# Two kinds of side work on ScalarE queued behind each tile's eviction, and one pair's late output operands behind the next pair's first copy

## The chip, the cores and the metric

The kernel runs on one NeuronCore of a Trainium2 chip. A core has a matmul engine (TensorE, PE), three engines for elementwise work (VectorE or DVE, ScalarE or ACT, GpSimd or POOL), a queue for DMA issues (SyncE, SP) and 16 DMA engines. Each engine takes its instructions in one fixed order and waits on semaphores for what the others make. Matmuls write to PSUM, eight banks of 2 KB per partition; the other engines carry ("evict") results from there to SBUF. The metric is the device time of one execution, in microseconds (us).

## The reference

One layer of a token mixer on two groups, 2048 latent tokens and 128 context tokens, width 1024. Each group is normalised and modulated, multiplied by one combined input projection and split over three branches (a gated delta rule over chunks, a spatial gating unit, Fourier mixing); the branches are gated, projected and merged:

```python
def mixer(xn, w_in, conv_w, a_log, dt_bias, ...):
    proj = jnp.einsum('btd,de->bte', xn, w_in)
    qkv, beta, dec, z_a, u_b, v_b, z_b, x_c, z_c, gates = jnp.split(proj, points, axis=-1)
    qkv = short_conv(qkv, conv_w).astype(jnp.float32)        # 3 taps, then SiLU
    q, k, v = jnp.split(qkv, 3, axis=-1)
    beta = jax.nn.sigmoid(beta...)
    g = -jnp.exp(a_log) * jax.nn.softplus(dec + dt_bias)     # log-decays
    o, s_f, s_b = delta_bidir(q, k, v, g, beta, s0_f, s0_b)  # needs exp(gam_i - gam_j)
    ...
    pb = jnp.einsum('btnw,nwd->btnd', br, w_branch)
    gt = jax.nn.sigmoid(gates.reshape(B, T, N_BRANCH, D_MODEL))
    merged = jnp.einsum('btnd,btnd->btd', gt, pb)
    return jnp.einsum('btd,de->bte', merged, w_out), s_f, s_b
```

## The kernel before

Products are made in float16 pairs: an operand x is held as a high and a low half (xh, xl; whi, wlo), and one product is three matmuls, high by high, low by high and high by low. The tokens stay in SBUF with channels on the partitions; 2176 tokens are cut into four tiles of 512 and one of 128 (TBS).

The stage that the change touches first makes q, k and v: a loop over 12 column tiles (ct) of the projection. For each of the five token tiles, `gemm_T` issues 24 matmuls (8 blocks of the contraction, three products each) into a PSUM bank, and L986 evicts the bank to `raw` on ScalarE at high priority. The banks are taken in turn from two pools of three (ps_d, ps_mm), so six evictions can be outstanding before TensorE has to wait. Behind the five tiles stands the column tile's convolution: one tap on ScalarE (L993), two on VectorE (L994, L995), a sigmoid in four pieces on ScalarE (L998), products on GpSimd (L999), a store (L1000), and for the q and k columns a square with a sum (L1002).

A column tile's weights come through a chain of their own: a DMA into wst (two buffers), the sum of squares on ScalarE (L317), its cast wscb on VectorE (L265), a matmul with ones, the scales on VectorE (L279 to L281), the high half whi on ScalarE (L329) and the low half wlo on VectorE (L330).

Beside this run two generators whose results the stage itself doesn't read:

- `decays()` makes the decay table `tok` out of the projection bdp (L838 to L872, with exponentials and a logarithm on ScalarE at L854, L859 and L861), its cumulative sums with a few matmuls on TensorE (which read tok), transposed copies of them (gr, L893) that are written to memory (gamR), and then 17 decay rows of 128x1024: loaded from gamR, two operations on VectorE (L924, L925), an exponential on ScalarE (L912) and a store. `pace` steps it as tiles are issued.
- `token_sums()` makes sums and differences of token blocks for the merge at the end of the program (products with seven instead of eight multiplications): additions on GpSimd and VectorE (L956 to L962), four casts to float16 on ScalarE (L965), the remainders (L966), and stores. One set has sums of 512 columns (sg, st), the other two stretches of 512 and 64 (sgs, sts); the program holds 32 casts of 512 and 16 of 64.

A list scheduler sets each engine's order from the program's order, priorities and readiness as it reckons them; `tc.issue_after(ins)` is an edge by which everything issued under it stands behind `ins` on that engine's queue.

Much later, the merge runs over eight pairs of column blocks (`last_merge`, L2081). A pair's first bank R is copied by ScalarE at L2129 with high priority; `held_back` holds the previous pair's last operands (pa, made by `quarters` at L935 and L936), and `step()` issues them when the third unit of the current pair begins.

Of the kernel before, what the change touches and what calls it, by code (L numbers as in the profile page):

```python
# [14 lines left out]
AF = mybir.ActivationFunctionType  # L15
# [180 lines left out]
def hybrid_flow_kernel(ctx: ExitStack, tc: tile.TileContext, x_prompt, x_sample, state_delta, c, c_ctx, w_ada,  # L196
# [628 lines left out]
    def decays():  # L825
# [83 lines left out]
            return row  # L909

        def flush(t, row):
            A.activation(row, row, AF.Exp)  # L912
            A.dma_start(decD[t], row.rearrange("p d h i -> p d (h i)"))

        xb = [None]
# [30 lines left out]
    def token_sums(*which):  # L946


        for p_ in which:
            a0, b0, cn, _ = QUADS[p_]  # L950
            a, b = slice(a0, a0 + cn), slice(b0, b0 + cn)
            for k in range(4):
                own, sg, st_ = (ep, "sg", "st") if cn == 512 else (a1p, "sgs", "sts")
                f11, f12, f21, f22 = [sb(own, [P, cn], sg, bufs=4) for _ in range(4)]
                for on, f, kk, ts in ((G, f21, k, b), (V, f11, k, a), (G, f22, k + 4, b), (G, f12, k + 4, a)):
                    on.tensor_tensor(f, xh[:, kk, ts], xl[:, kk, ts], ALU.add)  # L956
                yield 1
                V.tensor_tensor(f22, f21, f22, ALU.add)
                G.tensor_tensor(f21, f11, f21, ALU.subtract)
                yield 1  # L960
                V.tensor_tensor(f11, f22, f11, ALU.subtract)
                V.tensor_tensor(f12, f12, f11, ALU.subtract)  # L962
                for i, f in enumerate((f22, f11, f21, f12)):
                    st = sb(own, [P, 2, cn], st_, F16, bufs=3)
                    A.copy(st[:, 0], f)  # L965
                    (V if i % 2 else G).tensor_tensor(st[:, 1], f, st[:, 0], ALU.subtract)  # L966
                    SY.dma_start(sD[p_][:, i, :, k, :], st)
                    yield 1

    beside, small_sums = token_sums(1, 0), token_sums(2)  # L970
    flip = [0]
    pace.start(decays(), 6.0)
    for ct in range(12):
        w = getw(1, 2 if ct < 6 else min(4, 15 - ct))
        for half in range(1):
            raw = sb(a1p, [P, LP], "raw")
            G.memset(raw[:, 0:1], 0.0)
            G.memset(raw[:, NS + 1:NS + 3], 0.0)
            G.memset(raw[:, LP - 1:LP], 0.0)
            for t0, tn in TBS:  # L980
                flip[0] ^= 1
                ps = bank(ps_d if flip[0] else ps_mm, [P, tn])
                gemm_T(ps, w, 0, xh[:, :, t0:t0 + tn], xl[:, :, t0:t0 + tn])
                o = t0 + 1 if t0 < NS else t0 + 3
                with tc.high_priority():
                    A.activation(raw[:, o:o + tn], ps, AF.Copy, scale=w.inv)  # L986
                pace.tick(tn / 100)
                if ct:
                    next(beside if tn == 512 else small_sums, 0)
                    if tn < 512:  # L990
                        next(small_sums if ct > 4 else beside, 0)
            y = sb(a1p, [P, LP - 2], "cy")
            A.activation(y, raw[:, 0:LP - 2], AF.Copy, scale=convw(0, ct))  # L993
            V.scalar_tensor_tensor(y, raw[:, 1:LP - 1], convw(1, ct), y, ALU.mult, ALU.add)  # L994
            V.scalar_tensor_tensor(y, raw[:, 2:LP], convw(2, ct), y, ALU.mult, ALU.add)  # L995
            for c0 in range(0, LP - 2, CQ):
                c1 = min(c0 + CQ, LP - 2)
                A.activation(raw[:, 1 + c0:1 + c1], y[:, c0:c1], AF.Sigmoid)  # L998
                G.tensor_tensor(y[:, c0:c1], y[:, c0:c1], raw[:, 1 + c0:1 + c1], ALU.mult)  # L999
            G.dma_start(qkvD[ct], y)  # L1000
            if ct < 4 or ct > 7:
                A.activation(raw[:, 1:LP - 1], y, AF.Square, accum_out=vqs[:, ct:ct + 1])  # L1002
# [1078 lines left out]
    def last_merge(i, p_, w, after, ending):  # L2081


        a0, b0, cn, _ = QUADS[p_]
        a, b = slice(a0, a0 + cn), slice(b0, b0 + cn)
        js = (i, i + 4)
        mr = [sb(orp, [P, 2 * cn], "mr", bufs=4) for _ in js]
        for t, j in zip(mr, js):
            SY.dma_start(t, mD[j][:, a0:a0 + 2 * cn])
        tokens = lambda k, ts: [x[:, k:k + 4, ts] for x in x2]  # L2090
        small = p_ == 1
        if small:
            c0, d0, cs, _ = QUADS[2]
            c, d = slice(c0, c0 + cs), slice(d0, d0 + cs)
            pm = sb(orp, [P, 2, 2 * cs], "pm")
            for n_, j in enumerate(js):
                SY.dma_start(pm[:, n_], mD[j][:, c0:c0 + 2 * cs])
            p7 = bank(ps_x, [P, 7, cs])
        unit = [0]

        def step():
            if unit[0] == 2 and held_back:
                held_back.pop()()
            after(unit[0])
            unit[0] += 1

        def multiply(ps, w_, ts, fresh, n_, sum_=None):
            part(ps, w_, [sums[sum_, p_][:, l] for l in range(2)] if sum_ else tokens(*ts[0]), fresh)
            if small:
                part(p7[:, n_], w_, [sums[sum_, 2][:, l] for l in range(2)] if sum_ else tokens(*ts[1]))  # L2110
            step()

        def gated(n_, ts, c_):
            ps = bank(ps_d, [P, cn])
            part(ps, w.branch[n_], [o16[:, l, :, ts] for l in range(2)])
            with tc.high_priority():
                V.scalar_tensor_tensor(c_, ps, bi_[:, js[n_]:js[n_] + 1], c_, ALU.mult, ALU.mult)
            m_ = mr[n_][:, ts.start - a0:ts.stop - a0]
            G.tensor_tensor(m_, m_, c_, ALU.add)
            step()  # L2120
            return m_

        if not small:
            c = d = None
        R = bank(ps_mm, [P, cn])
        multiply(R, w.b11, ((0, a), (0, c)), True, 0)
        p1 = sb(ep, [P, cn], "sg", bufs=4)
        with tc.high_priority():
            A.copy(p1, R)  # L2129
        Y = bank(ps_mm, [P, cn])  # L2130
        multiply(Y, w.t2, None, True, 1, 1)
        u2 = sb(ep, [P, cn], "st", bufs=3)
        total(u2, Y, p1)
        multiply(R, w.b21, ((4, a), (4, c)), False, 2)
        c11 = sb(ep, [P, cn], "sg", bufs=4)
        sigmoid(c11, R, w)
        multiply(Y, w.t3, None, False, 3, 2)
        u3 = sb(ep, [P, cn], "st", bufs=3)
        total(u3, Y, p1)
        X = bank(ps_mm, [P, cn])  # L2140
        multiply(X, w.t1, ((0, b), (0, d)), True, 4)
        total(u3, X, u3)
        sigmoid(u3, u3, w)
        m1a = gated(0, a, c11)
        multiply(Y, w.t4, ((4, b), (4, d)), False, 5)
        total(p1, Y, p1)
        sigmoid(p1, p1, w)
        m2b = gated(1, b, u3)
        multiply(X, w.b22, None, False, 6, 3)
        total(u2, X, u2)  # L2150
        sigmoid(u2, u2, w)
        if ending:
            ending()
        m1b = gated(0, b, p1)
        quarters(i, b0, m1b, m2b)
        if small:
            q_ = sb(ep, [P, 7, cs], "sg", bufs=4)
            r_ = sb(ep, [P, 4, cs], "st", bufs=3)
            A.copy(q_.rearrange("p n c -> p (n c)"), p7.rearrange("p n c -> p (n c)"))
            for out, x, y in ((r_[:, 0], 0, 2), (q_[:, 1], 0, 1), (q_[:, 3], 1, 3), (r_[:, 1], 3, 5), (r_[:, 3], 3, 4), (q_[:, 4], 1, 4),  # L2160
                              (r_[:, 2], 4, 6)):
                G.tensor_tensor(out, q_[:, x], q_[:, y], ALU.add)
            sigmoid(r_.rearrange("p n c -> p (n c)"), r_.rearrange("p n c -> p (n c)"), w)
        m2a = gated(1, a, u2)
        held_back.append(lambda: quarters(i, a0, m1a, m2a))
        if small:
            ps = bank(ps_x, [P, 2, 2 * cs])
            for n_ in range(2):
                part(ps[:, n_], w.branch[n_], [o16[:, l, :, c0:c0 + 2 * cs] for l in range(2)])
            for n_ in range(2):  # L2170
                g_ = r_[:, 2 * n_:2 * n_ + 2].rearrange("p n c -> p (n c)")
                V.scalar_tensor_tensor(g_, ps[:, n_], bi_[:, js[n_]:js[n_] + 1], g_, ALU.mult, ALU.mult)
                G.tensor_tensor(pm[:, n_], pm[:, n_], g_, ALU.add)
                SY.dma_start(mD[js[n_]][:, c0:c0 + 2 * cs], pm[:, n_])
# [37 lines left out]
        SY.dma_start(gp[1], gateD[0:1, :].to_broadcast([P, D]))  # L2212
        scale_gate(gp[1], gp[1], winv)

    held_back = []
    for n_, (p_, i) in enumerate(order):
        nxt = pair_weights(order[n_ + 1][1], n_ > 2) if n_ < 7 else None

# [261 lines left out]
```

## Time and profile before

| | us |
|---|---|
| median of three runs | 2196.15 (2189.08 to 2197.21) |
| profiled execution, its own time | 2190.18 |
| its span | 2188.4 |
| mean granted clock of TensorE | 0.981 |
| ACT table loads of the decays' exponentials (L912) | 3 of 1.283 |
| qkv stage, first matmul of the second tile to the end of its last | 144.67 to 452.8 |

The span is the time from the first to the last instruction; busy shares are of it. In a group or timeline row, L251 is the helper that records every matmul of a product, so rows of that line are told apart by their tiles (`b<-xh,wlo` is the high half of the tokens by the low half of the weights into a bank). `[9.23 <-DVE tok L872]` behind a row says that the engine was idle for 9.23 us before it, and which instruction ended that.

### The profile page before, as it was taken

Reading aid. Unit: us, or ns where it says so; the run is one execution under the profiler, and the core shown is the slowest. Engines: PE = TensorE matmul, PEld = TensorE weight load, DVE = VectorE, ACT = ScalarE, POOL = GpSimd, SP = SyncE. Lnnn points to the kernel's source line nnn. Section 1 sums busy time; section 2 is a strip of 40 time slices with the busy share of each in tenths; the row PEclk is TensorE's granted clock in tenths of the full one; section 3 lists DMA queues with packets and bytes.
Section 4 is the critical chain, followed back from the end, with each engine's and each line's share of the span. In section 5 each row is a group of like instructions: output and inputs, shape, how many; then the busy total and the mean of one; then the engine's idle time right before and its main releaser. Section 6 shows DMA issues by size and latency. Waiting matters only on the chain.

```text
span 2188.4 us, 43365 instructions
## 1 busy us (share of the span) xinstructions
PE 2081.8 (95%) x16169; PEld 1190.6 (54%) x16169; DVE 1432.0 (65%) x2988; ACT 1116.4 (51%) x2525; POOL 965.4 (44%) x1178
## 2 busy tenths in 40 slices
PE   7997799999999999999899999999999998999997
PEld 4453344455555587768556655565565454444443
DVE  6667994448876777555667565766666567676345
ACT  5545675656565665355555455665665445222112
POOL 0346663324565655543423242345454435333454
PEclk9998899999999999999999999999999999999999
DMA  8523862237777575244657565776766785885862
GB/s 344 218 90 124 265 237 101 100 111 236 250 240 245 183 236 152 69 136 135 191 189 225 159 215 173 226 234 211 224 199 199 259 277 199 317 278 186 302 220 89
DMA packets 266211, 440.13 MB, mean 201 GB/s; under 512 B 47608, under 2 KB 148752, under 8 KB 262928
## 3 DMA queue, kind: packets, MB, share of 16 engines
q1 hardware_dynamic: 213488, 336.27, 47.4%
q0 software_dynamic: 12688, 57.04, 7.0%
q10 hardware_dynamic: 39824, 44.05, 6.0%
q8 instruction: 127, 2.08, 0.4%
q14 instruction: 84, 0.69, 0.1%
HBM read 276.61 MB, written 160.65 MB: 200 GB/s over the span
## 4 chain that ended last, share of the span: by engine, by line
PE 46%; DVE 9%; DMA 7%; issue 3%; ACT 3%; POOL 3%; SPq 0%; ACTq 0%; POOLq 0%; DVEq 0%
PE b L251 45%; DMA st<-br 2%; POOL E L1164 1%; DMA wst<-in_w_blk_dram 1%; DVE XB L1163 1%; DMA ei<-XB 1%; DVE big L1750 1%; DVE pa L936 1%; DMA br<-o 0%; DMA big<-pa 0%; DMA tw<-slot 0%; ACT big L1749 0%; DVE o L1297 0%; PE b L1065 0%; DMA wo<-slot 0%
## 5 line engine op out<-in xcount | busy, mean ns | idle before, releaser
L251 PE MATMUL b<-xh,whi 128*128 128x512 f16 (+2 forms) x1792 | 603.5, 347 | 14.7 <-ACT sg L2129 3.7
L251 PE MATMUL b<-xh,wlo 128*128 128x512 f16 (+2 forms) x1792 | 601.8, 347 | 11.3 <-DVE wlo L330 11.3
L251 PE MATMUL b<-xl,whi 128*128 128x512 f16 (+2 forms) x1792 | 604.0, 347 | 0.0
L251 PEld LDWEIGHTS <-whi 128*128 128x128 f16 x3872 | 348.4, 98 | 344.8 <-issue 34.7
L251 PEld LDWEIGHTS <-wlo 128*128 128x128 f16 x1936 | 189.8, 98 | 186.9 <-DVE wlo L330 12.5
L251 PE MATMUL b<-big,bhi 128*128 128x512 f16 (+1 forms) x960 | 252.7, 348 | 2.0 <-ACT big L1749 1.2
L251 PE MATMUL b<-big,blo 128*128 128x512 f16 (+1 forms) x480 | 162.8, 347 | 0.0
L251 PEld LDWEIGHTS <-xh 128*128 128x128 f16 x1512 | 119.7, 98 | 31.0 <-issue 1.6
L1164 POOL TENSOR_TENSOR E<-E,XB 128x31 f32<-128x31 f32 (+15 forms) x155 | 95.1, 613 | 76.2 <-DVE XB L1163 62.3
L251 PEld LDWEIGHTS <-bhi 128*128 128x128 f16 x960 | 86.8, 98 | 76.7 <-issue 2.8
L1237 POOL COPY T<-ES 32x256 f16<-32x256 f16 x68 | 30.7, 451 | 190.4 <-DMA ES<-ei 174.6
L999 POOL TENSOR_TENSOR cy<-cy,raw 128x545 f32<-128x545 f32 (+1 forms) x48 | 66.8, 1415 | 100.7 <-ACT raw L998 100.7
L251 PE MATMUL b<-whi,xl 128*128 128x128 f16 x544 | 94.5, 221 | 0.0
L251 PE MATMUL b<-whi,xh 128*128 128x128 f16 x544 | 94.5, 221 | 0.0
L251 PE MATMUL b<-wlo,xh 128*128 128x128 f16 x544 | 94.5, 221 | 0.0
L251 PEld LDWEIGHTS <-xl 128*128 128x128 f16 x824 | 74.7, 98 | 14.9
L1344 POOL TENSOR_TENSOR skn<-skn,ed 128x512 f32<-128x512 f32 x34 | 37.5, 1103 | 99.6 <-DMA skn<-kv 99.5
L1163 DVE TENSOR_TENSOR XB<-XB,E 128x31 f32<-128x31 f32 (+15 forms) x155 | 54.7, 353 | 40.8 <-POOL E L1164 39.8
L251 PEld LDWEIGHTS <-big 128*128 128x128 f16 x480 | 46.8, 98 | 60.1 <-DMA big<-pa 3.2
L330 DVE SCALAR_TENSOR_TENSOR wlo<-wst,wsc,whi 128x1024 f16<-128x1024 f32 x44 | 59.3, 1349 | 27.7 <-ACT whi L329 27.4
L251 PE MATMUL b<-xh,big 128*128 128x512 f16 x280 | 74.8, 379 | 2.2 <-DMA big<-pa 2.2
L1787 POOL TENSOR_TENSOR mrow<-mrow,sg 128x512 f32<-128x512 f32 (+1 forms) x40 | 48.3, 1211 | 61.2 <-DVE sg L1786 32.7
(578 smaller groups left out, 4805.0 us busy)
## 6 DMA issues: line engine op xcount, KB each, us to landing
wst<-in_w_blk_dram SPq DMA_DIRECT2D x58, 512.0 KB, 4.9
pa<-pa POOLq DMA_DIRECT2D x16, 896.0 KB, 5.2
qkv<-cy POOLq DMA_DIRECT2D x12, 1089.0 KB, 5.3
st<-br SPq DMA_DIRECT2D x48, 256.0 KB, 4.3
big<-pa SPq DMA_DIRECT2D x12, 896.0 KB, 8.6
dc<-dec SPq DMA_DIRECT2D x17, 512.0 KB, 6.1
kq<-qkv SPq DMA_DIRECT2D x34, 256.0 KB, 5.5
kv<-tok POOLq DMA_DIRECT2D x17, 512.0 KB, 4.9
```

The costliest lines, as they stand in the source:

```text
L251: newest[0] = PE.matmul(out, l, r, start=start, stop=stop, skip_group_check=reopened)
L330: w.low = V.scalar_tensor_tensor(w.lo, st, s, w.hi, ALU.mult, ALU.subtract)
L936: V.scalar_tensor_tensor(lo, src, s, hi, ALU.mult, ALU.subtract)
L999: G.tensor_tensor(y[:, c0:c1], y[:, c0:c1], raw[:, 1 + c0:1 + c1], ALU.mult)
L1163: V.tensor_tensor(t3, X3[:, 0:k, k:k + 1].to_broadcast([P, k, n_]), E3[:, k:k + 1, k:32].to_broadcast([P, k, n_]), ALU.mult)
L1164: G.tensor_tensor(E3[:, 0:k, k:32], E3[:, 0:k, k:32], t3, ALU.subtract)
L1237: G.tensor_copy(T16[rows(a0, b), :, :, b], ES[0:32, :, 2 * a0 + b, :, wT])
L1344: G.tensor_tensor(h3(kn_), h3(kn_), bc(ed[:, d, t, :], P), ALU.mult)
L1750: V.scalar_tensor_tensor(o16[:, 1, g, t0:t0 + tn], st, s, o16[:, 0, g, t0:t0 + tn], ALU.mult, ALU.subtract)
L1787: G.tensor_tensor(mr, mr, sg, ALU.add)
```

## The change

Three edges are added; no instruction of the computation is added or removed.

- The exponential of a decay row (`flush`) stands behind the newest eviction of the qkv stage at the time when the program issues it.
- So does each of the 48 casts of the token sums.
- The previous pair's held-back operands stand behind the copy of the current pair's first bank.

```diff
         def flush(t, row):
-            A.activation(row, row, AF.Exp)
+            with tc.issue_after(evicted[0].ins):
+                A.activation(row, row, AF.Exp)
             A.dma_start(decD[t], row.rearrange("p d h i -> p d (h i)"))
...
                     st = sb(own, [P, 2, cn], st_, F16, bufs=3)
-                    A.copy(st[:, 0], f)
+                    with tc.issue_after(evicted[0].ins):
+                        A.copy(st[:, 0], f)
...
+    evicted = [None]
     beside, small_sums = token_sums(1, 0), token_sums(2)
...
                 with tc.high_priority():
-                    A.activation(raw[:, o:o + tn], ps, AF.Copy, scale=w.inv)
+                    evicted[0] = A.activation(raw[:, o:o + tn], ps, AF.Copy, scale=w.inv)
...
             if unit[0] == 2 and held_back:
-                held_back.pop()()
+                with tc.issue_after(copied[0].ins):
+                    held_back.pop()()
...
         with tc.high_priority():
-            A.copy(p1, R)
+            copied[0] = A.copy(p1, R)
...
-    held_back = []
+    held_back, copied = [], [None]
```

Since the scheduler fills each engine's queue around these edges, other engines' orders move too. Line numbers of the new kernel are one higher behind L912, two or three higher from L965 on, and four higher at the merge.

VectorE, the end of the chain of the decay table (tok) in the first column tile. Before, with sums (sg, sgs of 512 and 64 columns) between its steps:

```order
L858 SCALAR_TENSOR_TENSOR tok_1701<-tok_1701 128x136
L958 TENSOR_TENSOR sgs_3681<-sgs_3680,sgs_3681 128x64
L860 TENSOR_SCALAR tok_1701<-tok_1701 128x136
L862 TENSOR_SCALAR tok_1701<-tok_1701 128x136
L863 RECIPROCAL tok_1701<-tok_1701 128x136
L961 TENSOR_TENSOR sg_2100<-sg_2103,sg_2100 128x512
L961 TENSOR_TENSOR sgs_3678<-sgs_3681,sgs_3678 128x64
L864 TENSOR_TENSOR tok_1701<-tok_1701 128x136
L962 TENSOR_TENSOR sg_2101<-sg_2101,sg_2100 128x512
L962 TENSOR_TENSOR sgs_3679<-sgs_3679,sgs_3678 128x64
L865 TENSOR_SCALAR tok_1701<-tok_1701 128x136
L966 TENSOR_TENSOR st_2213<-sg_2100,st_2213 128x512
```

and the same place in the changed kernel:

```order
L858 SCALAR_TENSOR_TENSOR tok_1701<-tok_1701 128x136
L860 TENSOR_SCALAR tok_1701<-tok_1701 128x136
L862 TENSOR_SCALAR tok_1701<-tok_1701 128x136
L863 RECIPROCAL tok_1701<-tok_1701 128x136
L864 TENSOR_TENSOR tok_1701<-tok_1701 128x136
L865 TENSOR_SCALAR tok_1701<-tok_1701 128x136
L866 TENSOR_TENSOR tok_1701<-tok_1701 128x136
L867 TENSOR_TENSOR tok_1701<-tok_1701 128x136
L868 SCALAR_TENSOR_TENSOR tok_1701<-tok_1701 128x136
L872 SCALAR_TENSOR_TENSOR tok_1701<-tok_1701,al_1705 128x68 x2
```

The sums have left the chain; they stand behind it, spread over later column tiles.

VectorE, in front of the low half of the fifth column tile's weights (wlo_275). Before (sg are sums, E and XB decay rows, cy a convolution):

```order
L958 TENSOR_TENSOR sg_418_3190<-sg_417_3189,sg_418_3190 128x512
L925 TENSOR_TENSOR E_309_2344<-E_309_2344,cst_1_87 128x1024
L924 TENSOR_TENSOR XB_325_2477<-XB_325_2477,tok_230_1701 128x1024 x2
L327 TENSOR_TENSOR winv_287_2140<-wsc_286_2136,xsc_89_382 128x1
L961 TENSOR_TENSOR sg_415_3187<-sg_418_3190,sg_415_3187 128x512
L925 TENSOR_TENSOR XB_325_2477<-XB_325_2477,cst_1_87 128x1024
L994 SCALAR_TENSOR_TENSOR cy_293_2217<-raw_271_2030,pc_8_101,cy_293_2217 128x2178
L925 TENSOR_TENSOR XB_325_2477<-XB_325_2477,cst_1_87 128x1024
L962 TENSOR_TENSOR sg_416_3188<-sg_416_3188,sg_415_3187 128x512
L330 SCALAR_TENSOR_TENSOR wlo_275_2063<-wst_239_1833,wsc_286_2136,whi_274_2062 128x1024
```

and in the changed kernel:

```order
L998 SCALAR_TENSOR_TENSOR cy_270_2016<-raw_237_1803,pc_8_101,cy_270_2016 128x2178
L968 TENSOR_TENSOR st_277_2068<-sg_251_1860,st_277_2068 128x512
L962 TENSOR_TENSOR sg_280_2100<-sg_283_2103,sg_280_2100 128x512
L963 TENSOR_TENSOR sg_281_2101<-sg_281_2101,sg_280_2100 128x512
L925 TENSOR_TENSOR dc_288_2142<-dc_288_2142,tok_230_1701 128x1024
L926 TENSOR_TENSOR dc_288_2142<-dc_288_2142,cst_1_87 128x1024
L265 CAST wscb_303_2302<-wss_299_2265 128x1
L279 TENSOR_SCALAR wsc_286_2136<-b_285_2134 128x1
L280 TENSOR_SCALAR wsc_286_2136<-wsc_286_2136 128x1
L281 TENSOR_SCALAR wsc_286_2136<-wsc_286_2136 128x1
L327 TENSOR_TENSOR winv_287_2140<-wsc_286_2136,xsc_89_382 128x1
L330 SCALAR_TENSOR_TENSOR wlo_275_2063<-wst_239_1833,wsc_286_2136,whi_274_2062 128x1024
```

The half stands ahead of the third column tile's convolution (raw_271) now, where it stood behind that convolution's first tap, and it has fewer sums and decay rows in front.

ScalarE, the third column tile (raw_2030 is its evictions' output). Before:

```order
L993 ACTIVATE cy_2016<-raw_1803,pc_101 128x2178
L912 ACTIVATE dc_1850<-dc_1850 128x1024
L317 ACTIVATE wlo_2264,wss_2265<-wst_2060 128x1024
L913 DMA dec_1284<-dc_1850 128x1024
L912 ACTIVATE dc_1853<-dc_1853 128x1024
L986 ACTIVATE raw_2030<-b_2034,winv_1699 128x512
L913 DMA dec_1285<-dc_1853 128x1024
L965 CAST st_2969<-sg_2889 128x512
L912 ACTIVATE E_1856<-E_1856 128x1024
L913 DMA dec_1286<-E_1856 128x1024
L986 ACTIVATE raw_2030<-b_2072,winv_1699 128x512
```

and in the changed kernel:

```order
L989 ACTIVATE raw_2030<-b_2034,winv_1699 128x512
L913 ACT_TABLE_LOAD
L913 ACTIVATE dc_1850<-dc_1850 128x1024
L967 CAST st_2068<-sg_1860 128x512
L914 DMA dec_1284<-dc_1850 128x1024
L989 ACTIVATE raw_2030<-b_2072,winv_1699 128x512
L1001 ACT_TABLE_LOAD
L1001 ACTIVATE raw_1803<-cy_2016 128x545 x3
L1001 ACTIVATE raw_1803<-cy_2016 128x543
L317 ACTIVATE wlo_2264,wss_2265<-wst_2060 128x1024
L989 ACTIVATE raw_2030<-b_2108,winv_1699 128x512
L329 ACTIVATE whi_2062<-wst_1833,wsc_2136 128x1024
```

One exponential and one cast follow an eviction, and the sigmoid of the tile before stands between two exponentials, each with a table load. Over the whole program ScalarE has 27 table loads where it had 15.

## The prediction

> **What bounds the kernel now.** I read the page first, then the waits of TensorE, then the stretches of the stage in which they lie, and last the timelines around the largest ones.
>
> ```profile
> PE 2081.8 (95%) x16169; PEld 1190.6 (54%) x16169; DVE 1432.0 (65%) x2988; ACT 1116.4 (51%) x2525; POOL 965.4 (44%) x1178
> ```
>
> TensorE is busy for 95% of the span of 2188.4 us, so about 107 us of idle time is all that a new order of work can take away, besides what a reduced clock costs. The list of what TensorE waited for says where it lies:
>
> ```profile
> PE b L251 <- DVE wlo L330: 11.3, 1, 11.3
> PE b L251 <- DVE tok L872: 9.8, 2, 9.2
> PE b L251 <- DVE wscb L265: 5.1, 4, 2.0
> ...
> PE b L251 <- ACT whi L329: 2.7, 1, 2.7
> ```
>
> The columns are total, times and longest. The two largest waits of the program, one for the low half of a weight block and one for the decay table, stand in the qkv stage, which the edits touch. Cut into stretches (stretch; length; busy us of PE, PEld, DVE, ACT, POOL; granted clock; DMA share), that stage reads:
>
> ```profile
> 144.67:220.00 75.33, 63.09 (x559) 33.84 (x557) 58.96 (x89) 41.80 (x74) 50.27 (x65) 0.91 0.43 135
> 220.00:275.00 55.00, 41.03 (x218) 19.45 (x217) 54.02 (x44) 34.79 (x45) 38.06 (x20) 0.88 0.80 261
> 275.00:330.00 55.00, 53.02 (x276) 24.97 (x275) 49.42 (x46) 38.79 (x51) 36.57 (x30) 0.97 0.67 232
> 330.00:385.00 55.00, 52.70 (x275) 24.89 (x273) 23.20 (x30) 28.30 (x42) 17.45 (x25) 0.97 0.27 100
> 385.00:452.80 67.80, 67.80 (x390) 33.62 (x388) 26.60 (x36) 40.06 (x54) 22.09 (x28) 1.00 0.28 105
> ```
>
> PE's five figures add to 277.6 of 308.1 us: 30.5 us idle. VectorE is full from 220 to 275 (54.02 of 55), nearly full to 330, and then works less than half the time. The stage is bound by VectorE's queue early and by TensorE late; work that VectorE does early for nobody in the stage delays what TensorE needs.
>
> ```profile
> 181.93 0.69 PE L251 MATMUL b<-tok,cst 128*128 128x68 f32 x2 [9.23 <-DVE tok L872]
> 184.20 0.63 PE L251 MATMUL b<-xh,whi 128*128 128x512 f16 x1
> 184.63 0.63 PE L251 MATMUL b<-xl,whi 128*128 128x512 f16 x1
> ...
> 266.33 0.61 PE L251 MATMUL b<-xh,wlo 128*128 128x512 f16 x1 [11.31 <-DVE wlo L330]
> ...
> 270.74 0.38 PE L251 MATMUL b<-xl,whi 128*128 128x512 f16 x1
> 270.95 0.38 PE L251 MATMUL b<-xh,wlo 128*128 128x512 f16 x1
> ```
>
> After both waits the matmuls start 0.43 us apart for a while, where 0.21 is normal (270.74 to 270.95). From 266.33 to 270.74 about ten of them run slow, and as many from 184.20: ten times 0.21 is 2.1 us, twice, **4.3 us** on top of the waits.
>
> What stood on VectorE just before the late low half:
>
> ```profile
> 262.31 2.17 DVE L925 TENSOR_TENSOR XB<-XB,cst 128x1024 f32<-128x1024 f32 x1
> 264.40 0.68 DVE L962 TENSOR_TENSOR sg<-sg,sg 128x512 f32<-128x512 f32 x1
> 265.00 1.27 DVE L330 SCALAR_TENSOR_TENSOR wlo<-wst,wsc,whi 128x1024 f16<-128x1024 f32 x1
> ```
>
> It is decay rows and token sums, neither of which this stage reads.
>
> **The decay table (9.8 us).** The table's chain on VectorE and ScalarE starts when its projection leaves TensorE, whose last matmul is
>
> ```profile
> 156.93 0.18 PE L251 MATMUL b<-bdp,xh 128*128 128x32 f16 x1
> ```
>
> and whose rows on VectorE are, with the first and the last of the sums' twelve that stand between them:
>
> ```profile
> 166.77 0.29 DVE L858 SCALAR_TENSOR_TENSOR tok<-tok 128x136 f32<-128x136 f32 x1
> 166.98 0.22 DVE L958 TENSOR_TENSOR sgs<-sgs,sgs 128x64 f32<-128x64 f32 x1
> ...
> 169.21 0.60 DVE L860 TENSOR_SCALAR tok<-tok 128x136 f32<-128x136 f32 x1 [2.01 <-ACT tok L859]
> 170.97 0.23 DVE L862 TENSOR_SCALAR tok<-tok 128x136 f32<-128x136 f32 x1 [1.16 <-ACT tok L861]
> ...
> 180.00 1.63 DVE L958 TENSOR_TENSOR sg<-sg,sg 128x512 f32<-128x512 f32 x1
> 181.55 1.55 DVE L872 SCALAR_TENSOR_TENSOR tok<-tok,al 128x68 f32<-128x68 f32 x2
> ```
>
> It took 26 us, to 183.1. In the new order nothing of the sums stands inside it on either engine. From L858 to the end the trace has 16.3 us, of which those twelve rows of the sums make about 7; the stretch from 156.93 to 166.77 was nearly all queue, and 2 us of real work (two adds, two scalings, two biases, each 0.2 to 0.5) are left of it. So the table is ready at about 157.1 + 2 + 9.3 = 168.4, up to 170 where a table load ends last. The matmuls that read it stand earlier too, in the first column tile's last, narrow token tile:
>
> ```profile
> 168.49 0.22 PE L251 MATMUL b<-xh,whi 128*128 128x128 f16 x1
> ```
>
> TensorE is there, and at the end of that tile soon after. I take a wait of 0.5 us (bounds 0 and 2) for 9.8: **-9.3**.
>
> **The weight halves (11.3 and 2.7) and the transposed rows (2.0).** In the new order the fifth column tile's low half stands 30 rows behind the second copy of the transposed decays (L893), before 45. In the trace that copy and the first decay row are
>
> ```profile
> 207.09 0.28 DVE L893 COPY gr<-b 68x128 f32<-68x128 f32 x1
> 214.44 2.36 DVE L924 TENSOR_TENSOR dc<-dc,tok 128x1024 f32<-128x1024 f32 x2 [2.35 <-DMA dc<-gamR]
> ```
>
> and the half came at 265.00. With the table 15 us sooner and no casts in front of its three exponentials, whose chain (one table load of 1.28, small steps of 0.2 to 0.9, one step of a convolution) is an estimate of some 11 us, I put that copy at about 179 and, with the same 7 us for the way over memory, the first decay row at 186. From there to the fourth tile's low half stand ten decay operations, two sums, one step of a convolution and the half itself. Decay operations have these bounds (shortest, median, longest):
>
> ```profile
> L924 DVE TENSOR_TENSOR dc<-dc,tok x8: 1214/1218/2174, 214.4 to 302.7; 128x1024 f32<-128x1024 f32 x8
> ```
>
> At 1.2 to 2.2 each they make 12 to 22; with 6 for the rest the half is ready between 204 and 214, at the middle value of 1.7 about 209. Without stalls a column tile takes 22 us (96 matmuls at 0.2155 and 24 at 0.056), so TensorE wants it at 168.7 + 0.5 + 44 = 213. That is the tightest place: no wait at the middle, 1 us at the upper end. The fifth tile's half follows thirteen rows on, some 13 us, at 222, and is wanted at 235. The waits of the stretch from 140 to 330 have one more row that goes, for the transposed decays:
>
> ```profile
> PE b L251 <- DVE gr L893: 2.0, 1, 2.0
> ```
>
> So 11.3, 2.7 and 2.0 (the wait for the transposed rows) go: **-16.0**, and the clock's **-4.3** with them. For the waits on wscb (5.1 in all) I count nothing: the matmuls that read it keep their rows and the column's scale still comes over DMA, ScalarE and VectorE.
>
> **What ScalarE pays.** Two kinds of work are spread out, the casts (here with the idle time before them, and what ended it) and the exponentials, which take a table load where the function before was another:
>
> ```profile
> L965 ACT CAST st<-sg 128x512 f16<-128x512 f32 x32 | 18.9, 612 | 21.2 <-DVE sg L958 7.5 <-DVE sg L961 7.2 <-issue 2.5
> ```
>
> ```profile
> L912 ACT ACT_TABLE_LOAD  x3: 1283/1283/1283, 239.9 to 305.1; - x3
> ```
>
> Now one or two stand behind each eviction until the last column tile, so an exponential alternates with the sigmoid of a convolution and 12 more table loads are issued: 12 x 1.283 = 15.4 us. ScalarE's five figures above add to 183.7 us; with 15.4 that is 199 of the some 278 us that the stage would take, 16.6 of 23 per column tile. The cover is real but not wide: an eviction may come late by the banks, six in all. The trace shows how much that allows:
>
> ```profile
> 229.45 0.22 PE L251 MATMUL b<-xh,wlo 128*128 128x128 f16 x1
> 248.02 0.36 ACT L986 ACTIVATE raw<-b,winv 128x128 f32<-128x128 f32 x1
> ```
>
> The third tile's last bank, filled at about 229.5, was emptied at 248.0, and TensorE ran on. With 18 us of room I cost the loads at **0** (bounds 0 and 15.4, if ScalarE becomes the pace).
>
> Another view of that price, which the sum doesn't use: these rows show a load taking 1.28 us and the exponential behind it starting at once.
>
> ```profile
> 167.57 1.28 ACT L859 ACT_TABLE_LOAD   x1
> 168.86 0.32 ACT L859 ACTIVATE tok<-tok 128x136 f32<-128x136 f32 x1
> ```
>
> The Trainium skill, "ScalarE: Activation LUTs", What ACT_TABLE_LOAD costs, gives 1283 ns and a drain of about 1380 for every switch, and the section on table sets advises doing all of one set before the next, which this change undoes. By that price twelve loads would be 32 us and ScalarE would have 216 of 278; the trace agrees with the first figure and shows no drain at this place, and the sum would stay, but it is the rule that speaks for rival A.
>
> **The merge.** A pair's first copy stood behind four operands of the pair before:
>
> ```profile
> 1835.12 1.10 ACT L935 ACTIVATE pa<-mr,msc 128x512 f16<-128x512 f32 x2
> 1836.13 0.56 ACT L2129 COPY sg<-b 128x512 f32<-128x512 f32 x1
> ```
>
> In the new order the two operands of the first row stand behind the copy; the two ahead of them, made of sums, stay. That is 1.0 us sooner where TensorE waited, a few tenths elsewhere: **-1**. The operands' stores are read one pair later, far behind.
>
> **What comes later.** The stage's last convolution is now followed by the last small casts (0.24 us each) and by stores that used to be out by 325. On SyncE's queue the cached states' load waits for the last decay row and stands ahead of four stores and of a weight block for the next stage, which is read behind the stage's last weights. The stage after it changes its order only locally. I take **+1** for the tail and **+1** for later stages (bounds -3 and +25).
>
> The sum: -9.3 - 16.0 - 4.3 - 1 + 1 + 1 = about **-29** on the profiled execution's own 2190.2, so 2161. Those runs' median, 2196, lies 6 above it; a new kernel's median would lie between, and I say 2162.
>
> **The rivals.**
>
> A. *ScalarE becomes the pace.* Behind each eviction stands a cast or an exponential, and one whose sum isn't ready holds all evictions behind it. For it: 12 more table loads, the full 15.4 us. Against it: 16.6 of 23 us. It gives 2162 + 15 = **2177**.
>
> B. *The waits move.* VectorE's work is the same, and the fourth tile's low half has only 4 us of room; a chain 8 us later than I put it gives a wait of 4 us or more, a slow clock behind it, and the same once more for a later half. 2162 + 11 (half of 9.3 + 11.3) gives about **2173**. For it: VectorE at 54.02 of 55. Against it: 15 rows fewer in front.
>
> C. *Slower.* ScalarE in order, blocked by sums: a cast waits for VectorE and GpSimd, they for the two or three buffers that the casts free, and evictions wait behind all. To lose the 29 and 11 more, evictions have to be late by 18 + 40 = 58 us within the stage, about 5 us in each of twelve tiles beyond the idle 6 us: some 130 us of blocked time. Before the 32 large casts it was 21.2 us in all, in the row above; it would have to be six times that. It gives **2207** or more.
>
> D. *Given back later.* The sums and decay rows land up to 50 us later in the program's work while the stage ends 30 sooner. If the loads of decay rows come too late for the scan, or GpSimd and DMA set the pace behind the stage, TensorE waits there for what it saved: **2190**, no change. The first product of the scan stage
>
> ```profile
> L1065 PE MATMUL b<-cst,kq x136: 272/273/308, 478.0 to 834.6; 128*128 128x128 f32 x136
> ```
>
> starts 25 us behind the stage's end, at about 448 in the new time; by the new order the last decay row leaves in the tenth column tile, at about 370. That is 78 us of room.
>
> **How the numbers follow.** Forecast 0.58, A 0.13, B 0.14, C 0.06, D 0.09. A measurement of this kernel can tell about 0.5% (11 us) from no change. Faster by more than that: the forecast, B and nearly all of A, less the forecast's own upper tail, **0.81**; within: D and a little of A and B, **0.13**; slower: **0.06**. The range: downward the whole idle time of the stage and its clock (35), with later stages at their better end and the lower runs, 2147; upward B and A with the upper bounds of the loads and some of D, 2188.
>
> **What would show it.** Right: no wait over 3 us on L872 and L330, the granted clock at 0.97 or more from 170 to 280, the casts ending near the stage's end, 27 table loads, the last eviction at about 424 instead of 453. Wrong: TensorE waiting for banks (releaser ACT raw on L986's successor), a new wait on whi or wlo at about 213 (B), or the delta stage longer by what the first stage saves (D).

## The result and the profile after

The changed kernel is slower by half a per cent: a median of 2204.13 us over six runs against 2193.73 us over six of the kernel before, ratio 1.0049 with a 95% interval from 1.0036 to 1.0062. The profiled span went from 2188.4 to 2204.1 us, 15.7 us more; the medians differ by 10.4, since the execution profiled before lies 3.5 us below its median and the one after 1.8 above. The forecast was 2162 us, in a range of 2147 to 2188.

TensorE has the same work and idles longer, by the first line of the page:

```profile
PE 2082.0 (94%) x16169; PEld 1188.8 (54%) x16169; DVE 1421.6 (65%) x2988; ACT 1130.4 (51%) x2537; POOL 965.9 (44%) x1178
```

The list of what TensorE waited for (total, times, longest) from 140 to 480 us shows that the rows which the forecast was about are gone, and that others stand in their place:

```profile
PE b L251 <- DVE wscb L265: 16.9, 2, 14.6
PE b L251 <- ACT v4hi L329: 10.0, 1, 10.0
PE b L251 <- ACT raw L989: 6.5, 1, 6.5
PE b L251 <- DVE wlo L330: 2.3, 1, 2.3
PE b L251 <- DVE v4lo L330: 1.7, 1, 1.7
```

The decay table's 9.8 us and the transposed rows' 2.0 have no row any more, and the low half's 11.3 shrank to 2.3. (v4hi and v4lo are the two halves of the next stage's first weights.) The same five stretches of the qkv stage as before (busy us of PE, PEld, DVE, ACT, POOL; granted clock; DMA share) say where the gain was made and where it was lost:

```profile
144.67:220.00 75.33, 75.33 (x664) 41.07 (x662) 48.59 (x66) 39.01 (x57) 28.11 (x32) 1.00 0.33 113
220.00:275.00 55.00, 55.00 (x295) 26.43 (x294) 30.08 (x36) 40.85 (x54) 30.36 (x33) 1.00 0.47 166
275.00:330.00 55.00, 43.94 (x228) 20.57 (x227) 45.26 (x46) 30.83 (x45) 34.09 (x30) 0.94 0.51 164
330.00:385.00 55.00, 40.35 (x217) 19.35 (x216) 37.40 (x45) 35.26 (x51) 27.66 (x28) 0.88 0.53 186
385.00:452.80 67.80, 59.10 (x330) 28.99 (x329) 37.22 (x45) 43.53 (x58) 38.07 (x35) 0.97 0.44 150
```

Until 275 TensorE doesn't stop at all, at full clock: 130.3 us busy where it was 104.1, **26 us won**. From 275 to 452.8 it is idle for 34.4 us where it was idle for 4.3, **30 us lost**, and the clock falls with it. VectorE's early rush (54.02 of 55 busy) is spread out now, 30 to 45 of 55, to the stage's end.

Not all of the 30 us belong to the stage's own products. TensorE starts the last of them at 443.88, 9 us sooner than before, and then waits 10 us for the next stage's weights:

```profile
443.88 0.22 PE L251 MATMUL b<-xh,wlo 128*128 128x128 f16 x1
454.06 0.59 PE L251 MATMUL b<-v4hi,xh 128*128 128x512 f16 x1 [9.96 <-ACT v4hi L329]
```

Before, it went on at once:

```profile
452.85 0.22 PE L251 MATMUL b<-xh,wlo 128*128 128x128 f16 x1
...
453.35 0.38 PE L251 MATMUL b<-v4hi,xh 128*128 128x512 f16 x1
```

The first product of the scan stage then starts at 489.1 where it was 478.0. So between the stage's last product and the scan the changed kernel loses 20 us: 15.4 in four waits (v4hi 10.0, wsscb 2.4, v4lo 1.7, kq 1.3), and nearly 3 in matmuls that start 0.43 us apart, at a granted clock of 0.50 from 456.75 to 462.30. ScalarE ends its part late as well: the last eviction comes at 464.3 instead of 453.1. Measured by that, the stage ends 11.2 us later and 4.5 us are lost behind it; measured by TensorE's products, it ends 9 us sooner, with its late waits, and the loss comes behind it.

The first of the late losses, read from the timelines (start, length, engine, line; in brackets the engine's idle time before and what ended it):

```profile
278.88 1.22 DVE L925 TENSOR_TENSOR XB<-XB,tok 128x1024 f32<-128x1024 f32 x1 [6.44 <-DMA XB<-gamR]
...
281.22 2.17 DVE L330 SCALAR_TENSOR_TENSOR wlo<-wst,wsc,whi 128x1024 f16<-128x1024 f32 x1
...
283.42 0.33 SPq L293 DMA_DIRECT2D wst<-in_w_blk_dram  x1
...
286.64 1.06 ACT L317 ACTIVATE wlo<-wst 128x1024 f16<-128x1024 f32 x1 [8.54 <-DMA wst<-in_w_blk_dram]
...
296.07 1.28 ACT L1001 ACT_TABLE_LOAD   x1 [7.20 <-DVE cy L998]
...
299.57 0.67 ACT L989 ACTIVATE raw<-b,winv 128x512 f32<-128x512 f32 x1
...
300.29 0.58 PE L251 MATMUL b<-xh,whi 128*128 128x512 f16 x1 [6.53 <-ACT raw L989]
```

A decay row comes late from memory, so VectorE stands before it; the low half of a weight block stands behind it; the block's staging buffer comes free only with that half, so the next weights' load goes out at 283.42; ScalarE, in order, waits 8.5 us for that load, then 7.2 us for the convolution that VectorE did meanwhile, with all evictions queued behind; and TensorE runs out of banks. The second loss has another path:

```profile
347.27 4.25 DVE L925 TENSOR_TENSOR XB<-XB,tok 128x1024 f32<-128x1024 f32 x2
...
352.58 0.15 DVE L279 TENSOR_SCALAR wsc<-b 128x1 int32<-128x1 int32 x1
...
353.96 1.15 ACT L329 ACTIVATE whi<-wst,wsc 128x1024 f16<-128x1024 f32 x1 [9.84 <-DVE wsc L280]
...
358.20 1.04 ACT L317 ACTIVATE wlo<-wst 128x1024 f16<-128x1024 f32 x1
...
359.58 0.16 PE L251 MATMUL b<-wscb,ones 128*128 128x1 bf16 x1 [14.65 <-DVE wscb L265]
```

The scales of one block (L279, 0.15 us of work) stand on VectorE behind decay rows; ScalarE waits 9.8 us for them with its high half, and the next block's sum of squares, for which TensorE has a matmul queued, stands behind that. The third, in front of the next stage, is of the same kind, with a convolution in the place of the decay rows. Its taps on VectorE hold the scales of v4hi until 448, and ScalarE does the convolution's sigmoid, an eviction and a cast before the high half:

```profile
444.95 3.26 DVE L998 SCALAR_TENSOR_TENSOR cy<-raw,pc,cy 128x2178 f32<-128x2178 f32 x1
448.13 0.15 DVE L279 TENSOR_SCALAR wsc<-b 128x1 int32<-128x1 int32 x1
...
448.29 1.28 ACT L1001 ACT_TABLE_LOAD   x1 [4.81 <-DVE wsc L279]
...
452.86 1.15 ACT L329 ACTIVATE v4hi<-wst,wsc 128x1024 f16<-128x1024 f32 x1
```

The groups of ScalarE (busy and mean, then idle time before) show how its waits for weights grew; from 144 to 470 us the high halves of the stage's own weights now cost

```profile
L329 ACT ACTIVATE whi<-wst,wsc 128x1024 f16<-128x1024 f32 x9 | 10.3, 1144 | 23.4 <-DVE wsc L280 23.4
```

where they had 2.5 us of idle time before them.

### The profile page after: what moved, and what is told of

Its sections match the earlier page's. It is cut to its first block, busy times and chain, and to the rows that moved or that the text cites. A ratio compares the mean times of both kernels' runs of the same rounds, so it can differ in the third digit from the quotient of the medians.

```text
span 2204.1 us, 43315 instructions
## 1 busy us (share of the span) xinstructions
PE 2082.0 (94%) x16169; PEld 1188.8 (54%) x16169; DVE 1421.6 (65%) x2988; ACT 1130.4 (51%) x2537; POOL 965.9 (44%) x1178
## 4 chain that ended last, share of the span: by engine, by line
PE 41%; DMA 9%; DVE 9%; ACT 4%; POOL 4%; issue 4%; SPq 1%; ACTq 0%; POOLq 0%; DVEq 0%
PE b L251 41%; DMA st<-br 2%; DMA ES<-ei 1%; POOL E L1167 1%; DVE XB L1166 1%; DMA ei<-XB 1%; DMA wst<-in_w_blk_dram 1%; DVE pa L937 1%; POOL st L1518 1%; DMA big<-pa 0%; DMA br<-o 0%; DVE big L1753 0%; DVE slot L937 0%; ACT nd L1118 0%; ACT big L1752 0%
## 5 line engine op out<-in xcount | busy, mean ns | idle before, releaser
L329 ACT ACTIVATE whi<-wst,wsc 128x1024 f16<-128x1024 f32 x44 | 50.3, 1144 | 41.8 <-DVE wsc L280 40.8
```

The source lines that it names most:

```text
L329: w.made = A.activation(w.hi, st, AF.Copy, scale=s)
```

## The experiments

My theory after the result was a **ring**: both kinds of side work now last through the whole stage, so each late weight block has to pass three in-order queues (SyncE, ScalarE, VectorE) that hold side work which itself waits for evictions. Its rivals were the **table loads**, and the **merge** for what was lost behind the stage. Ratios are to the kernel before, with 95% intervals; "last" is the start of the stage's last eviction on ScalarE (453.1 before), "next" the start of TensorE's first product with v4hi (453.3 before).

| run | ratio | interval | last | next |
|---|---|---|---|---|
| the change | 1.0049 | 1.0036 to 1.0062 | 464.3 | 454.1 |
| e1_casts: casts' edge alone | 0.9941 | 0.9926 to 0.9956 | 433.7 | 431.8 |
| e2_exps: exponentials' edge alone | 1.0056 | 1.0042 to 1.0069 | 466.7 | 460.2 |
| e3_merge: held-back operands alone | 1.0005 | 0.9996 to 1.0014 | 454.8 | 455.1 |
| e4_sigmoid: the change, 20 table loads fewer | 1.0028 | 1.0013 to 1.0043 | 451.1 | 440.9 |
| e5_weights_first: the change, weights ahead everywhere | 1.0007 | 0.9996 to 1.0018 | 443.9 | 437.5 |
| e6_pace3: the change, decays stepped twice as often | 0.9989 | 0.9977 to 1.0001 | 442.6 | 437.9 |
| e7_casts5: casts' edge in five column tiles | 0.9973 | 0.9957 to 0.9989 | 452.7 | 453.0 |
| e8_casts7: in seven | 0.9949 | 0.9937 to 0.9961 | 443.9 | 444.1 |
| e11_casts10: in ten | 0.9924 | 0.9906 to 0.9942 | 435.2 | 428.7 |
| e9_stage_weights: the change, weights ahead in this stage | 0.9991 | 0.9978 to 1.0005 | 444.9 | 438.5 |
| e10_weights_only: no edge, weights ahead in this stage | 1.0101 | 1.0081 to 1.0121 | 467.5 | 467.7 |
| e12_casts_weights: casts' edge and weights ahead | 0.9949 | 0.9932 to 0.9966 | 437.2 | 437.0 |

**Each edge alone.** The first leaves the casts' edge and takes the other two out:

```diff
         def flush(t, row):
-            with tc.issue_after(evicted[0].ins):
-                A.activation(row, row, AF.Exp)
+            A.activation(row, row, AF.Exp)
...
             if unit[0] == 2 and held_back:
-                with tc.issue_after(copied[0].ins):
-                    held_back.pop()()
+                held_back.pop()()
```

> Only the casts of the token sums carry their edge; exponentials and held-back operands are queued as before (13 table loads). Ring theory (both kinds of side work, stretched over the whole stage, hold the late weights' chains in the in-order queues of SyncE, ScalarE and VectorE): the decays are done early again, only sums are late, so the early waits are gone and part of the late ones stays away: 5 to 20 us less than before, 2174 to 2189. Table theory (12 more table loads hold the evictions): no price is left and the whole early gain stays: about 2164. Merge theory (the merge's edge costs): no statement on the stage.

Measured 2181.4 us, inside the ring's bounds: **the casts' edge gains 0.6%**. The decays run early again (last exponential of the dc rows at 269.8 where it was 311.3), and TensorE's waits in the stage are down to

```profile
PE b L251 <- ACT raw L988: 6.9, 2, 3.6
PE b L251 <- DVE wscb L265: 6.1, 2, 4.2
```

The second run keeps the exponentials' edge alone (the merge's edge is out, as above):

```diff
-                    with tc.issue_after(evicted[0].ins):
-                        A.copy(st[:, 0], f)
+                    A.copy(st[:, 0], f)
```

> Only the decay rows' exponentials carry their edge (27 table loads); casts as before. Ring theory: the wait on the decay table (9.8 us) is back, since the sums stand in its chain again, and the decay rows run late: 0 to 12 us more than before, 2193 to 2206. Table theory: all the price without the gain, 15 us or more above before, 2208 or higher.

2205.6 us, as slow as the change: the loss comes with this edge. Its waits join the old early one and the new late ones:

```profile
PE b L251 <- DVE wscb L265: 13.1, 3, 9.4
PE b L251 <- DVE tok L872: 9.8, 2, 9.3
PE b L251 <- ACT raw L988: 8.4, 4, 4.4
```

The third keeps the merge's edge alone (both other edges out, as above).

> Only the held-back operands stand behind the next pair's copy. By my forecast 1 us less than before (2192 to 2193). Merge theory (the 4.5 us that the changed kernel loses behind the qkv stage come from here): 3 to 5 us more, 2197 to 2199.

No difference that can be measured. The wait that the edge was aimed at went from 3.7 to 1.1 us, and the ones behind it grew. From 1750 to 2010 us it reads

```profile
PE b L251 <- DVE st L2076: 6.2, 3, 3.7
PE b L251 <- DVE sg L1787: 5.1, 1, 5.1
...
PE b L251 <- ACT sg L2131: 1.1, 1, 1.1
```

where before had 4.2, 2.6 and 3.7: VectorE's sums of the next banks are late next. The merge doesn't explain the 4.5 us behind the stage.

**Table loads.**

```diff
             with tc.issue_after(evicted[0].ins):
-                A.activation(row, row, AF.Exp)
+                A.activation(row, row, AF.Sigmoid)
```

> The changed kernel with the sigmoid in place of the decay rows' exponential: this part computes another function, the order of every engine's instructions is the same, and 20 of the 27 table loads (25.7 us of ScalarE) are gone. Table theory: evictions come sooner and the time falls by 15 us or more, to 2189 or less. Ring theory: ScalarE's idle time only moves, within 5 us of the changed kernel, 2199 to 2206.

The time lies inside the ring's bounds and far from the table theory's, but in the stage both were partly right. Its last eviction comes 13 us sooner than with the change (451.1), and so does the next stage's first product, so the loads do cost there, about half of the 25.7 us that went; but the whole program only gains 4.5 us (2199.6 against 2204.1). The loads hold some of the 30 us lost from 275 on and not the larger part of the difference to e1.

**Weights ahead of side work, and decays sooner.** The first puts the cast of the sum, the scales and both halves of every weight block at high priority:

```diff
-        sb16 = widened(ss, wp, "wsc")
+        with tc.high_priority():
+            sb16 = widened(ss, wp, "wsc")
...
+        with tc.high_priority():
             s, inv = scales(None, wp, "wsc", sb16)
...
+        with tc.high_priority():
             w.made = A.activation(w.hi, st, AF.Copy, scale=s)
             w.low = V.scalar_tensor_tensor(w.lo, st, s, w.hi, ALU.mult, ALU.subtract)
```

> The changed kernel with the cast, scales and both halves of each weight block at high priority on VectorE and ScalarE. If the loss comes from weight chains standing behind sums and decay rows on these two queues, most of the late waits go: 2184 to 2196. If the weights are late further up (their loads behind stores and row loads on SyncE, or the two staging buffers), it stays within 4 us of the changed kernel, 2200 to 2208.

The other steps the decays twice as often, with all edges in place:

```diff
-    pace.start(decays(), 6.0)
+    pace.start(decays(), 3.0)
```

> The changed kernel with the decays' generator stepped twice as often (quota 3.0 for 6.0), the edges as they are: the last exponential stands some 120 places earlier on ScalarE and there are 17 table loads. If the exponentials' edge costs because it pins the decay rows to the program's pace, so that they run until the stage's end, the loss mostly goes: 2180 to 2194. If an exponential behind every eviction costs by itself, wherever it stands: 2200 or more.

Both bring the last eviction 20 to 22 us forward (443.9 and 442.6 against 464.3), and the next stage's first product by 16 to 17. In the first, TensorE doesn't wait for banks or halves any more; beside one wait of 5.4 us for a load of the next stage there is only

```profile
PE b L251 <- DVE wscb L265: 19.0, 6, 4.9
```

six waits of up to 4.9 us; in the second, the last exponential of the decay rows comes at 307.1 where it was 438.8, though one wait of 10.9 us for a bank stays. So most of the loss needs both: decay rows that last to the stage's end, and weight chains that stand behind them. It isn't the number of exponentials behind evictions as such.

A run with the priority in the qkv stage alone (switched on before its loop and off behind it) was to show that the later stages have no part in this:

> The changed kernel with the weight blocks' cast, scales and halves at high priority in the qkv stage alone. Queue theory (the loss of the stage is weight chains behind sums and decay rows on VectorE and ScalarE): the last eviction at 440 to 448 as in the run with the priority everywhere, where it was 464. The later stages keep the changed kernel's order, which gives back 4 to 10 us: 2183 to 2196.

Last eviction 444.9, as expected; the median of 2190.1 is within noise of before (its profiled execution took 2198.6). And the same priority without any edge:

> The kernel of before, without any edge, with the weight blocks' cast, scales and halves at high priority in the qkv stage. If the early waits of before were mostly a matter of the weight chains' place on VectorE, this alone brings the waits of 11.3 and 2.7 and their slow clock: 2175 to 2185. If they need the sums out of the way: 2188 to 2196. The wait on the decay table (9.8) stays in both.

Neither: 1.0101, slower by 1%. The waits on the halves are gone, but priority for the weights doesn't replace taking the sums out of the way: the wait on the decay table is still there (9.5 us), and the waits on wscb grew to 26.6. I had expected a gain or nothing. With the casts' edge the priority doesn't add either:

> The casts' edge over the whole stage with the weight blocks first in the qkv stage. Queue theory: the remaining waits on wscb and on evictions (13 us with the casts' edge alone) go down too, last eviction at 425 to 432; with the scan stage's order as in the run with the casts alone, which gives back 10: 2170 to 2182.

Last eviction 437.2 where the casts alone had 433.7, so later and not sooner. The waits for banks (6.9) are gone, but those on wscb grew from 6.1 to 19.9 us. They are near that size in every run with weights ahead (19.0, 19.2, 26.6, 19.9); what makes them grow was not followed up.

**What is given back behind the stage.** e1 ends its stage 19.4 us sooner than before by the last eviction, and its program only 6.7 us, by the two profiled spans (2181.7 and 2188.4; the medians differ by 12). Most of the loss lies between the last product of the scan's first part (L1065) and the first output row (L1297). The casts' edge changes the order there, though it names nothing there: as I read it, the scheduler reckons the sums later and fills the engines' queues otherwise. By the traces' names (without buffer numbers), 1,622 of TensorE's 16,169 matmuls differ between e1 and before at their place in the order, most of them between 500 and 1000 us, and only 64, all before 200 us, when the edge is dropped behind a certain column tile:

```diff
                 with tc.high_priority():
-                    evicted[0] = A.activation(raw[:, o:o + tn], ps, AF.Copy, scale=w.inv)
+                    out = A.activation(raw[:, o:o + tn], ps, AF.Copy, scale=w.inv)
+                if ct < 5:
+                    evicted[0] = out
```

(on top of e1; 7 and 10 in the two others).

> Only the casts' edge, and only while the first five column tiles run (later casts stand behind the fifth tile's last eviction and are in effect free). Behind the qkv stage TensorE's order is then that of before. Order theory (the casts' edge to the stage's end shifts the scheduler's reckoning and so the order of the scan stage, which gives back some 10 of the 19 us that the casts' edge wins): the solve of the last chunk group takes 64 us again where it took 74, and the time is 2165 to 2177. Slack theory (the scan stage is bound by another chain and gives back whatever comes early): 2178 to 2187.

> As the run with five tiles, with seven. Order theory: 2165 to 2177, the stage's end as with the full edge (434) or a few us later. Slack theory: 2178 to 2187.

> Only the casts' edge, while the first ten column tiles run; TensorE's order behind the stage is that of before. Order theory: the stage ends as with the full edge or a little later (434 to 442) and nothing is given back: 2172 to 2181. Slack theory: 2180 to 2186.

Five was too few: the later casts run off at once (the last large one at 361.7) and the profiled stage gains nothing (452.7; that execution took 2192.2 us, and the median is 2184.8). With seven it gains 9, with ten 18, and neither gives it back behind that. The times of the first two, 2184.8 and 2181.8, miss the order theory's range and fall into the slack theory's, since their stages gained less than I took for granted; with ten the time lies in the order theory's range alone. These are the rows of that stretch, from the last L1065 to the first L1297, of before, of e1 and of e11:

```profile
834.60:993.00 158.40, 147.90 (x1960) 119.14 (x1958) 98.60 (x240) 74.63 (x186) 84.71 (x133) 0.97 0.41 117
```

```profile
817.00:985.40 168.40, 149.54 (x1959) 119.97 (x1957) 96.26 (x238) 74.29 (x183) 82.82 (x133) 0.96 0.40 111
```

```profile
816.80:976.00 159.20, 147.48 (x1950) 118.89 (x1948) 99.43 (x239) 74.18 (x185) 83.28 (x132) 0.97 0.40 116
```

The same 1,950 or so matmuls start at the same time in e1 and e11, and need 168.4 or 159.2 us (e11's row comes at 976.5, so its window is 0.5 us short): 18.9 us idle, or 11.7. In e1 the largest of the waits in it is

```profile
PE b L251 <- DMA ES<-ei: 6.6, 2, 4.3
```

the solved blocks' way over memory, for which the lists of e11 and before have no row. In the changed kernel this row is 4.4 us. The other runs agree: with the order of before the stretch takes 158.0 to 159.7 us (e2, e3, e7, e8, e10, e11), with e1's order in it 161.1 to 168.5 (the change, e4, e6, e9, e12). e5, whose order differs more, takes 145.0 and gives that back later, so what is shown is that the order decides, not which order is best. With ten column tiles the kernel takes 2174.9 us, ratio 0.9924, **below both kernels** (the interval overlaps e1's, so the times alone don't place it below e1); its stage's last eviction is

```profile
L988 ACT ACTIVATE raw<-b,winv x60: 348/671/692, 144.3 to 435.2; 128x512 f32<-128x512 f32 x48, 128x128 f32<-128x128 f32 x12
```

## Why the prediction was wrong

- **What bounds the kernel before** held: the two waits and their slow clock were there to be taken, and the change took them. No wait over 3 us on the table or the low halves is left, the clock is 1.00 to 275, and the 26 us won by then lie near the 29 forecast. With its last product TensorE is still 9 us ahead.
- **The step that failed** is the one on the weights: "For the waits on wscb (5.1 in all) I count nothing: the matmuls that read it keep their rows and the column's scale still comes over DMA, ScalarE and VectorE." That matmuls keep their rows says nothing of when their operand comes. I walked the chains of the fourth and fifth column tiles, where side work was taken away, and not those of the later ones, to which it was moved. Before, side work was nearly over by 320 and the later chains met half-empty queues (VectorE 23.20 of 55 busy); after, the first two losses shown met decay rows, and the one in front of the next stage a convolution and casts. The waits on wscb alone are 16.9 us; with v4hi, evictions and low halves they add to 37.4 us from 140 to 480, where the sum had left the 5.1 of before (4.3 of it in this stretch).
- **The cover for ScalarE** was counted as busy time (16.6 of 23 us per column tile) and as room of 18 us in the banks. The busy time was about right (189.5 us in the five stretches, where I had 199); but an in-order queue has idle time because something at its head waits, and that time is no room for what stands behind. ScalarE idled 8.5, 7.2 and 9.8 us at three of the places shown, with evictions queued. The loads, costed at 0 with 15.4 as upper bound, took 13 us of the stage by e4, which takes out 20 of them and not only the 12 that the change added.
- **Rival C** had the mechanism's kind (ScalarE blocked, evictions behind) and the wrong queue: I priced it by the casts' own waits for sums, 21.2 us before, and after the change the casts wait for no sum at all (3.7 us of idle time in all, for stores). What blocked at the places shown were a load of weights, scales and convolutions, late through VectorE and SyncE. By its price it needed six times the old waits; the ring needed only that both sides wait on each other.
- **Rival D** was right in part, with another cause. TensorE did give back behind the stage what it had won in it, but for weights of the next stage and not for decay rows: 9 us ahead at its last product, it is 11 behind at the scan's first. I gave the scan 78 us of room for late rows, and no decay row was late there; what cost 3 us in the changed kernel (161.3 us for the stretch that took 158.4) and 10 in e1 was the order.
- **The merge**: its wait fell by 2.6 us and not 1.0, and the gain went to the next waits.
- The rule of the Trainium skill, "ScalarE: Activation LUTs", Table sets: the hidden batching unit, on doing all of one table set before the next, pointed the right way: the edge that undid it is the one that loses. A large share of that loss doesn't need fewer loads to go away: e5 brings the last eviction 20 us forward with all 27 of them.

What stays open: how the ring's loss divides among SyncE's, ScalarE's and VectorE's queues, since undoing one link frees the others too, so that e4's 13, e5's 20 and e6's 22 us of a 30 us difference can't be added; and why e4 keeps 4.5 of its 13 us while its order of matmuls is the changed kernel's (in the profiled executions it is 12 us ahead at the last product of the scan's first part, 9.5 at the first output row and 5.5 at the end). Moving the row loads off SyncE's queue was not tried.

## What to carry to other kernels

When side work is moved out of the way of early waits, follow it to where it goes, and walk the critical operand chains there, into the next stage's first weights too: here, work that had run early for nobody had left the later queues half empty. Take a stage's end from the engine that bounds it: the last eviction came 11 us later while TensorE's last product came 9 us sooner. Of two kinds of side work, it paid here to spread the one with light steps (casts) and let the one with long steps, buffers that turn over memory and another table (decay rows) finish early. An edge that is given to a scheduler can change the order of stages that the edge doesn't name: compare those orders, and drop the edge where it has done its work.

## What the runs showed of the hardware

No drain shows around the table loads of ScalarE here. In the changed kernel an exponential starts as the load's 1.28 us end:

```profile
300.65 0.69 ACT L989 ACTIVATE raw<-b,winv 128x512 f32<-128x512 f32 x1
301.35 1.28 ACT L913 ACT_TABLE_LOAD   x1
302.65 1.06 ACT L913 ACTIVATE dc<-dc 128x1024 f32<-128x1024 f32 x1
```

The Trainium skill, "ScalarE: Activation LUTs", What ACT_TABLE_LOAD costs, adds about 1380 ns of drain to each switch; here the eviction before ends at 301.34 and the load starts at 301.35, so the trace disagrees, and this switch costs 1.28 us of ScalarE's time.
